# Seven half-size block products in place of eight in two feed-forward layers

## The chip, the cores and the metric

The kernel runs as one program on one core of one Trainium2 chip. The core has a matrix engine (TensorE; PE in the rows, PEld where it loads weights), a vector engine (DVE), a scalar engine (ACT), a general engine (POOL) and a queue engine (SP) that issues most of the transfers from device memory. Each engine works through its own instructions in their order and waits for the others by semaphores. Matmul results land in PSUM, which has eight banks of 128 x 512 fp32; everything else the engines touch lies in SBUF. The metric is the device time of one execution in microseconds (us).

## The reference: what is computed

Three transformer blocks run one after the other on 512 tokens of width 1024, in fp32. Each ends in a feed-forward layer of inner width 2816. The change touches that of block 2 (its second one) and that of block 3:

```python
def swiglu(h, w1, w2):                       # block 2
    g, u = jnp.split(h @ w1, 2, axis=-1)
    return (jax.nn.silu(g) * u) @ w2

def swiglu_3(u, w_gate, w_up, w_down):       # block 3
    return (jax.nn.silu(u @ w_gate) * (u @ w_up)) @ w_down

s = s + 0.5 * gate * swiglu(modulate(rmsnorm(s, nw), shift, scale), w1, w2)     # block 2
h = h + swiglu_3(rmsnorm_3(h, ffn_norm_g[l]), w_gate[l], w_up[l], w_down[l])    # block 3
```

## The kernel before

Activations lie with the channel on the 128 partitions and the 512 tokens along the row: a width of 1024 is eight tiles of 128 x 512. Every fp32 operand of a product is split in two: `hi`, the value cast to the matmul type fp32r (ACT), and `lo`, what the cast left (DVE, `lo = x - hi`). One product is then three matmuls (`mm3`, L280 to L282): hi by hi, hi by lo, lo by hi.

The up and gate projections go by pairs: `ffn` takes one tile of 128 gate channels and one of 128 up channels at a time, 22 pairs, in two parts of 11. For a pair, `wpair` (through `wload`, L260 to L265) brings 1 MB of weights as the tile `raw` (two buffers), and splits it into two chunks `wh`/`wl` of 128 x 1024 (three buffers each, `HL`). `gemm8` then makes each of the two 128 x 512 outputs from 8 x 3 matmuls of 512 columns in one PSUM bank. In block 2 ACT applies silu to the gate (L950), DVE multiplies by the up half (L951), and the result is split into the pair `g` (L318, L319). In block 3 (`kind` 3) both outputs are first multiplied by `A3`, the norm's factor per token (L954, L955). After 11 pairs the down projection runs: eight outputs of 11 x 3 matmuls of 512 columns, with weights through `wst`; then the other 11 pairs and the down projection again.

The activations `h` are eight hi/lo pairs of 128 x 512. In block 2 `modulated` makes them after the norm's statistics: a multiplication on DVE (L505), the cast with a shift on ACT (L508), the rest on DVE (L509), tile after tile. In block 3 `scaled` (L1557, L1558) makes them as the residual tiles of the projection before come out, since A3 is applied later.

A scheduler places the instructions of all engines by priority and dependence before the program runs; their order within an engine is then fixed. Tiles with few buffers decide how far one pair can run ahead of another.

## Time and profile before

| | us |
|---|---|
| median of 3 runs | 3245.63 (3242.1 to 3245.69) |
| the profiled execution | 3247.38 |
| its span, first to last instruction | 3245.4 |
| up and gate loads of block 2's layer, first to last issue | 2130.1 to 2436.5 |
| up and gate loads of block 3's layer, first to last issue | 2812.6 to 3130.7 |

In the rows, an instruction stands with its engine, the line of the kernel that issued it, its operation, and `out<-in` by the program's tile names (mm and x are PSUM banks, h the activations, wh and wl the weights' halves, raw the weights as loaded, tmp and ny scratch). Columns of a matmul are the second number of its shape. A busy PE is not a measure of its speed, because recorded matmuls overlap: what one costs is the distance between two starts.

### The profile page before, as it was taken

Reading aid. Unit: us, or ns where it says so; the run is one execution under the profiler, and the core shown is the slowest. Engines: PE = TensorE matmul, PEld = TensorE weight load, DVE = VectorE, ACT = ScalarE, POOL = GpSimd, SP = SyncE. Lnnn points to the kernel's source line nnn. Section 1 sums busy time; section 2 is a strip of 40 time slices with the busy share of each in tenths; the row PEclk is TensorE's granted clock in tenths of the full one; section 3 lists DMA queues with packets and bytes.
Section 4 is the critical chain, followed back from the end, with each engine's and each line's share of the span. In section 5 each row is a group of like instructions: output and inputs, shape, how many; then the busy total and the mean of one; then the engine's idle time right before and its main releaser. Section 6 shows DMA issues by size and latency. Waiting matters only on the chain.

```text
span 3245.4 us, 40565 instructions
## 1 busy us (share of the span) xinstructions
PE 3168.7 (98%) x15785; PEld 2608.5 (80%) x15785; DVE 2152.6 (66%) x3835; ACT 1202.7 (37%) x1891; POOL 46.7 (1%) x127
## 2 busy tenths in 40 slices
PE   8999999998999999999999999899999999999998
PEld 4888888888888889888888787678888877888886
DVE  6999697769775668765638766763334798454343
ACT  3343333435443335422225433532223327432222
POOL 0000000001000000000000000000000001100000
PEclk9999999999999999999999999999999999999999
DMA  6434433353635335554524211022222220022322
GB/s 241 153 122 132 135 129 99 110 183 124 204 132 160 109 114 175 167 173 146 184 88 162 78 65 53 16 89 90 94 99 85 92 69 27 27 91 84 105 84 79
DMA packets 117296, 370.37 MB, mean 114 GB/s; under 512 B 11120, under 2 KB 13680, under 8 KB 114672
## 3 DMA queue, kind: packets, MB, share of 16 engines
q1 hardware_dynamic: 108576, 356.21, 32.9%
q10 hardware_dynamic: 8528, 11.57, 1.1%
q8 instruction: 124, 2.03, 0.3%
q14 instruction: 68, 0.56, 0.1%
HBM read 365.64 MB, written 2.10 MB: 113 GB/s over the span
## 4 chain that ended last, share of the span: by engine, by line
PE 88%; DVE 6%; ACT 2%; DMA 2%; issue 1%; ACTq 0%; POOL 0%; DVEq 0%; POOLq 0%
PE mm L280 25%; PE mm L282 25%; PE mm L281 25%; DVE wl L265 2%; PE x L852 1%; PE mm L1634 1%; PE mm L825 1%; PE mm L824 1%; PE mm L826 1%; PE x L1286 1%; PE x L427 1%; PE x L1608 1%; PE mm L365 1%; PE x L435 1%; ACT wh L264 1%
## 5 line engine op out<-in xcount | busy, mean ns | idle before, releaser
L264 ACT CAST wh<-raw 128x1024 fp32r<-128x1024 f32 (+2 forms) x583 | 567.7, 975 | 1485.0 <-PE mm L281 1066.1
L280 PE MATMUL mm<-h,wh 128*128 128x512 f32 (+1 forms) x2488 | 976.7, 393 | 8.1 <-ACT hv L1249 2.1
L282 PE MATMUL mm<-h,wl 128*128 128x512 f32 (+1 forms) x2488 | 971.0, 390 | 1.8 <-DVE wl L265 1.8
L281 PE MATMUL mm<-h,wh 128*128 128x512 f32 (+1 forms) x2488 | 966.5, 389 | 1.1 <-DVE h L502 1.1
L265 DVE TENSOR_TENSOR wl<-raw,wh 128x1024 fp32r<-128x1024 f32 (+2 forms) x583 | 657.7, 1129 | 368.7 <-ACT wh L264 362.1
L280 PEld LDWEIGHTS mm<-h,wh 128*128 128x128 f32 x2488 | 469.5, 189 | 107.7 <-ACT hv L1249 2.6
L282 PEld LDWEIGHTS mm<-h,wl 128*128 128x128 f32 x2488 | 468.5, 188 | 106.8 <-DVE wl L265 3.1
L281 PEld LDWEIGHTS mm<-h,wh 128*128 128x128 f32 x2488 | 468.7, 188 | 102.0 <-DVE h L502 1.6
L282 PE MATMUL mm<-g,wl 128*128 128x512 f32 (+1 forms) x880 | 328.9, 374 | 2.3 <-DVE wl L265 2.2
L280 PE MATMUL mm<-g,wh 128*128 128x512 f32 (+1 forms) x880 | 329.1, 374 | 0.2 <-ACT wh L264 0.2
L281 PE MATMUL mm<-g,wh 128*128 128x512 f32 (+1 forms) x880 | 328.3, 373 | 0.0
L342 DVE SCALAR_TENSOR_TENSOR acc<-graw,cs,acc 128x512 f32<-128x512 f32 x252 | 186.2, 747 | 105.7 <-DMA graw<-w_mod 91.3
L282 PEld LDWEIGHTS mm<-g,wl 128*128 128x128 f32 x880 | 165.7, 188 | 35.6 <-DVE wl L265 3.3
L280 PEld LDWEIGHTS mm<-g,wh 128*128 128x128 f32 x880 | 165.7, 188 | 32.4 <-ACT wh L264 0.4
L281 PEld LDWEIGHTS mm<-g,wh 128*128 128x128 f32 x880 | 165.8, 188 | 32.0
L874 DVE SCALAR_TENSOR_TENSOR ca<-ap,pv,ca 128x512 f32<-128x512 f32 x232 | 173.2, 747 | 6.1 <-ACT ca L866 3.7
L280 PE MATMUL mm<-hc,wh 128*128 128x256 f32 x440 | 125.3, 285 | 4.5 <-DVE tmp L951 4.5
L281 PE MATMUL mm<-hc,wh 128*128 128x256 f32 x440 | 125.5, 285 | 0.0
L282 PE MATMUL mm<-hc,wl 128*128 128x256 f32 x440 | 125.1, 284 | 0.0
L951 DVE TENSOR_TENSOR tmp<-tmp,mm 128x512 f32<-128x512 f32 (+1 forms) x66 | 39.1, 596 | 99.8 <-PE mm L282 99.1
L280 PEld LDWEIGHTS mm<-hc,wh 128*128 128x128 f32 x440 | 84.0, 191 | 4.8 <-DVE tmp L951 4.7
L318 ACT CAST g<-tmp 128x512 fp32r<-128x512 f32 (+1 forms) x110 | 63.3, 577 | 63.5 <-DVE tmp L951 30.5
(596 smaller groups left out, 3941.8 us busy)
## 6 DMA issues: line engine op xcount, KB each, us to landing
graw<-w_mod SPq DMA_DIRECT2D x192, 256.0 KB, 3.1
raw<-f1u SPq DMA_DIRECT2D x44, 1024.0 KB, 5.0
raw<-w1s SPq DMA_DIRECT2D x32, 1024.0 KB, 5.0
raw<-f1d SPq DMA_DIRECT2D x32, 704.0 KB, 4.2
raw<-wup SPq DMA_DIRECT2D x22, 1024.0 KB, 5.0
raw<-f2u SPq DMA_DIRECT2D x22, 1024.0 KB, 4.9
raw<-f3u SPq DMA_DIRECT2D x22, 1024.0 KB, 4.9
raw<-w2s SPq DMA_DIRECT2D x17, 1024.0 KB, 4.9
```

What stands on the lines that cost most here:

```text
L264: nc.scalar.copy(hi[:, :cn], raw[:, c0:c0 + cn])
L265: nc.vector.tensor_sub(lo[:, :cn], raw[:, c0:c0 + cn], hi[:, :cn].bitcast(F32))
L280: mm(ps, hi, xh, start=first, stop=False)
L281: mm(ps, hi, xl, start=False, stop=False)
L282: mm(ps, lo, xh, start=False, stop=last)
L318: s.nc.scalar.copy(hi, src)
L342: nc.vector.scalar_tensor_tensor(accs[i], src, vec[:, k:k + 1], accs[i], op0=ALU.mult, op1=ALU.add)
L365: nc.tensor.matmul(ps, vec[:, k:k + 1], raw[:, q * 512:(q + 1) * 512], start=k == 0, stop=k == KD - 1)
L427: nc.tensor.matmul(ps[:, j * P:(j + 1) * P], col[:, j:j + 1].to_broadcast([P, P]), s.ident, start=True, stop=True)
L435: nc.tensor.transpose(ps[:, j * P:(j + 1) * P], x[:, j * P:(j + 1) * P], s.ident)
L874: nc.vector.scalar_tensor_tensor(ca, ap[:, i:i + T], s.v("conv_w", 8 * i + j), ca, op0=ALU.mult, op1=ALU.add)
L951: nc.vector.tensor_mul(sg, sg, pb)
```

## The change

The 2 x 2 block form of the product is used: the weights of a pair are four blocks (gate tile and up tile, each by the lower and upper half of the 1024 input channels), the activations four (lower and upper half of the channels, first and second 256 tokens). Strassen's scheme in Winograd's form gets the four output blocks from seven block products instead of eight, with sums of blocks before and after.

- `seven_in` makes seven sets of activations for each of four channel-tile pairs (b11, b21, t1, t2, m3, t4, m22; 128 x 256, hi and lo): four POOL subtractions of 256 columns, casts on ACT, remainders on DVE. It takes the place of `modulated` in block 2 and of `scaled` in block 3.
- `seven_weights` makes four sums s1 to s4 of the weight blocks by four POOL additions of 128 x 512 a pair, into `ws` (s2, s3) and `wt` (s1, s4), which have one buffer each, and splits seven blocks of 512 columns in four chunks: [a1 a2], [s2 s3], [b2 s1], [s4]. The three `wh` and three `wl` buffers stay.
- `seven` makes the seven products, each of 4 x 3 matmuls of 256 columns, and combines them on DVE (L1045 to L1052 of the new code) with one copy on ACT (`p1`, L1044).
- In block 3 the up half is multiplied by A3 on POOL (L944), the gate half on DVE (L943).

```diff
--- before.py
+++ after.py
@@ -937,6 +937,15 @@
         for i in range(NH):
             s.bg(bg(i))
             j = part * NH + i
+            if isinstance(h[0], dict):
+                sg, bt = s.seven(s.lp, w1, 2 * j, h)
+                if kind == 3:
+                    nc.vector.tensor_mul(sg, sg, s.A3)
+                    nc.gpsimd.tensor_mul(bt, bt, s.A3)
+                nc.scalar.activation(sg, sg, AF.Silu)
+                nc.vector.tensor_mul(sg, sg, bt)
+                g.append(s.split(sg, pool, "g", 2 * NH + 2, n))
+                continue
             w = s.wpair(w1, 2 * j)
             pa, pb = s.gemm8(w[0], h, n), s.gemm8(w[1], h, n)
             if kind == 1:
@@ -962,6 +971,86 @@
             for hi, lo, k, c in s.wst(w2, m, part * NH, NH):
                 s.mm3(ps, hi[:, c:c + P], lo[:, c:c + P], g[k][0], g[k][1], k == 0, k == NH - 1)
             out(m, ps)
+
+
+    HB = T // 2
+
+    def seven_in(s, pool, tp, y0, y1):
+
+        nc, g, H = s.nc, s.nc.gpsimd, s.HB
+        a, b = slice(0, H), slice(H, T)
+        (bh, bl), (th, tl) = s.hpair(), s.hpair()
+        mh, ml = (pool.tile([P, 3, H], F32R, tag="hs", name=s.nm("hs"), bufs=8) for _ in range(2))
+        t = tp.tile([P, 4, H], F32, tag="tt", name=s.nm("tt"), bufs=2)
+        nc.scalar.copy(bh[:, a], y0[:, a])
+        nc.vector.tensor_sub(bl[:, a], y0[:, a], bh[:, a].bitcast(F32))
+        g.tensor_sub(t[:, 1, :], y0[:, b], y0[:, a])
+        g.tensor_sub(t[:, 0, :], y1[:, b], t[:, 1, :])
+        g.tensor_sub(t[:, 2, :], y0[:, b], y1[:, b])
+        g.tensor_sub(t[:, 3, :], y1[:, a], t[:, 0, :])
+        t01, t23 = (t[:, i:i + 2, :].rearrange("p a f -> p (a f)") for i in (0, 2))
+        nc.scalar.copy(th, t01)
+        nc.vector.tensor_sub(tl, t01, th.bitcast(F32))
+        nc.scalar.copy(bh[:, b], y1[:, a])
+        nc.vector.tensor_sub(bl[:, b], y1[:, a], bh[:, b].bitcast(F32))
+        m01h, m01l = (m[:, 0:2, :].rearrange("p a f -> p (a f)") for m in (mh, ml))
+        nc.scalar.copy(m01h, t23)
+        nc.vector.tensor_sub(m01l, t23, m01h.bitcast(F32))
+        nc.scalar.activation(mh[:, 2, :], y1[:, b], AF.Copy, scale=-1.0)
+        nc.vector.scalar_tensor_tensor(ml[:, 2, :], y1[:, b], -1.0, mh[:, 2, :].bitcast(F32), op0=ALU.mult, op1=ALU.subtract)
+        return {"b11": (bh[:, a], bl[:, a]), "b21": (bh[:, b], bl[:, b]), "t2": (th[:, a], tl[:, a]), "t1": (th[:, b], tl[:, b]),
+                "m3": (mh[:, 0, :], ml[:, 0, :]), "t4": (mh[:, 1, :], ml[:, 1, :]), "m22": (mh[:, 2, :], ml[:, 2, :])}
+
+    def seven_weights(s, pool, name, mt):
+
+        nc, g = s.nc, s.nc.gpsimd
+        raw = s.wp.tile([P, 2048], F32, tag="raw", name=s.nm("raw"), bufs=2)
+        nc.sync.dma_start(raw.rearrange("p (m f) -> p m f", m=2), s.a[name][mt:mt + 2].rearrange("m p f -> p m f"))
+        a1, a2, b1, b2 = (raw[:, 512 * i:512 * i + 512] for i in range(4))
+        ws = pool.tile([P, 1024], F32, tag="ws", name=s.nm("ws"), bufs=1)
+        wt = pool.tile([P, 1024], F32, tag="wt", name=s.nm("wt"), bufs=1)
+        s2, s3, s1, s4 = ws[:, 0:512], ws[:, 512:1024], wt[:, 0:512], wt[:, 512:1024]
+        g.tensor_add(s1, b1, b2)
+        g.tensor_add(s2, a1, s1)
+        g.tensor_add(s3, a1, b1)
+        g.tensor_add(s4, a2, s2)
+        out = []
+        for parts in ([raw[:, 0:1024]], [ws], [b2, s1], [s4]):
+            hi = s.wp.tile([P, 1024], F32R, tag="wh", name=s.nm("wh"), bufs=HL)
+            lo = s.wp.tile([P, 1024], F32R, tag="wl", name=s.nm("wl"), bufs=HL)
+            c = 0
+            for src in parts:
+                n = src.shape[1]
+                nc.scalar.copy(hi[:, c:c + n], src)
+                nc.vector.tensor_sub(lo[:, c:c + n], src, hi[:, c:c + n].bitcast(F32))
+                c += n
+            out += [(hi, lo, o) for o in range(0, c, 512)]
+        return out
+
+    def seven(s, pool, name, mt, hs):
+
+        nc, V, H = s.nc, s.nc.vector, s.HB
+        a1, a2, s2, s3, b2, s1, s4 = s.seven_weights(pool, name, mt)
+        def prod(ps, w, mv):
+            hi, lo, o = w
+            for k in range(4):
+                c = o + k * P
+                s.mm3(ps, hi[:, c:c + P], lo[:, c:c + P], *hs[k][mv], k == 0, k == 3)
+            return ps
+        p1 = pool.tile([P, H], F32, tag="p1", name=s.nm("p1"), bufs=2)
+        at = s.tmp()
+        bt = pool.tile([P, T], F32, tag="bt", name=s.nm("bt"), bufs=2)
+        u, v = at[:, H:], bt[:, H:]
+        nc.scalar.copy(p1, prod(s.psm((P, H)), a1, "b11"))
+        V.tensor_sub(u, p1, prod(s.psx((P, H)), s2, "t2"))
+        V.tensor_add(at[:, 0:H], p1, prod(s.psm((P, H)), a2, "b21"))
+        V.tensor_sub(v, prod(s.psx((P, H)), s3, "m3"), u)
+        V.tensor_add(bt[:, 0:H], v, prod(s.psm((P, H)), b2, "t4"))
+        q = prod(s.psx((P, H)), s1, "t1")
+        V.tensor_add(v, v, q)
+        V.tensor_sub(u, u, q)
+        V.tensor_sub(u, u, prod(s.psm((P, H)), s4, "m22"))
+        return at, bt
 
     def dwconv3(s, pool, ps, j, n):
         nc = s.nc
@@ -1524,7 +1613,6 @@
         nc, tc = s.nc, s.tc
         A, _ = s.stats(acc["sq"], None, EPS2)
         sc = s.scw("scl3", s.v("n3w", 0, 8), s.modL[:, 56:64])
-        h = s.modulated(x, A, None, sc, s.modL[:, 48:56])
         hg = s.half_gate("hgl3", s.modL[:, 64:72])
         w = s.ct([P, 8], "w3")
         nc.vector.tensor_mul(w, s.v("fn2", 0, 8), s.v("an3", 0, 8))
@@ -1535,8 +1623,20 @@
             s.accum_w(acc, k, x[k], s.v("fn2", k))
             s.u.append(s.scaled(x[k], w[:, k:k + 1], NM))
         with tc.tile_pool(name="f3", bufs=1, reuse_waits="tile") as pool:
+            h = []
+            with tc.tile_pool(name="f3i", bufs=1, reuse_waits="tile") as tp:
+                for k in range(4):
+                    y = []
+                    for i in (k, k + 4):
+                        y.append(tp.tile([P, T], F32, tag="yy", name=s.nm("yy"), bufs=4))
+                        nc.vector.scalar_tensor_tensor(y[-1], x[i], sc[:, i:i + 1], A, op0=ALU.mult, op1=ALU.mult)
+                        nc.scalar.activation(y[-1], y[-1], AF.Identity, scale=1.0, bias=s.modL[:, 48 + i:49 + i])
+                    h.append(s.seven_in(pool, tp, *y))
+            s.lpc = tc.tile_pool(name="f3s", bufs=1, reuse_waits="tile")
+            s.lp = s.lpc.__enter__()
             s.ffn(pool, h, T, "f2u", "f2d", 2, s.part(x, hg), 0)
             s.ffn(pool, h, T, "f2u", "f2d", 2, out, 1)
+            s.lpc.__exit__(None, None, None)
         return x, acc
 
     def accum_w(s, acc, k, x, w):
@@ -1649,17 +1749,27 @@
             s.mixer3(pool, x, acc)
             acc = {}
             s.proj2("wo3", 1, s.o[4:8], s.part(x, 1.0, acc))
-        h = [s.scaled(x[k], s.v("ffn3", k)) for k in range(KD)]
         with tc.tile_pool(name="f4", bufs=1, reuse_waits="tile") as pool:
+            h = []
+            with tc.tile_pool(name="f4i", bufs=1, reuse_waits="tile") as tp:
+                for k in range(4):
+                    y = []
+                    for i in (k, k + 4):
+                        y.append(tp.tile([P, T], F32, tag="yy", name=s.nm("yy"), bufs=4))
+                        nc.scalar.activation(y[-1], x[i], AF.Copy, scale=s.v("ffn3", i))
+                    h.append(s.seven_in(pool, tp, *y))
             A, _ = s.stats(acc["sq"], None, EPS2)
             s.A3 = pool.tile([P, T], F32, tag="A3", name="A3")
             nc.scalar.copy(s.A3, A)
+            s.lpc = tc.tile_pool(name="f4s", bufs=1, reuse_waits="tile")
+            s.lp = s.lpc.__enter__()
             acc = {}
             def fin(k, ps):
                 s.resid(x[k], ps, 1.0, acc, k)
                 nc.scalar.activation(x[k], x[k], AF.Copy, scale=s.v("fn3", k))
             s.ffn(pool, h, T, "f3u", "f3d", 3, s.part(x, 1.0), 0)
             s.ffn(pool, h, T, "f3u", "f3d", 3, fin, 1)
+            s.lpc.__exit__(None, None, None)
         A, _ = s.stats(acc["sq"], None, EPS2)
         for k in range(KD):
             nc.vector.tensor_mul(x[k], x[k], A)
```

On DVE a pair of block 2 before is four rows. They stand here from the sixth pair on, with what surrounds them; wl is the remainder of a weight chunk, tmp the gated product, g its remainder:

```order
L319 TENSOR_TENSOR g_18167<-tmp_18163,g_18166 128x512
L265 TENSOR_TENSOR wl_18244<-raw_18237,wh_18243 128x1024
L951 TENSOR_TENSOR tmp_18230<-tmp_18230,mm_18205 128x512
L265 TENSOR_TENSOR wl_18307<-raw_18304,wh_18306 128x1024
L319 TENSOR_TENSOR g_18234<-tmp_18230,g_18233 128x512
L265 TENSOR_TENSOR wl_18311<-raw_18304,wh_18310 128x1024
L951 TENSOR_TENSOR tmp_18297<-tmp_18297,mm_18272 128x512
```

The same place now: the combination of one pair (tmp and bt are its two outputs, p its copied first product) lies between the remainders of the next pair's weights:

```order
L1046 TENSOR_TENSOR tmp_18666<-p_3383_18665,mm_18696 128x256
L1025 TENSOR_TENSOR wl_18662<-wt_18642,wh_18661 128x512
L1047 TENSOR_TENSOR bt_18667<-x_18710,tmp_18666 128x256
L1025 TENSOR_TENSOR wl_18782<-raw_18773,wh_18781 128x1024
L1048 TENSOR_TENSOR bt_18667<-bt_18667,mm_18724 128x256
L1050 TENSOR_TENSOR bt_18667<-bt_18667,x_18738 128x256
L1051 TENSOR_TENSOR tmp_18666<-tmp_18666,x_18738 128x256
L1025 TENSOR_TENSOR wl_18786<-ws_18775,wh_18785 128x1024
L1052 TENSOR_TENSOR tmp_18666<-tmp_18666,mm_18753 128x256
L1025 TENSOR_TENSOR wl_18790<-raw_18773,wh_18789 128x512
L1025 TENSOR_TENSOR wl_18790<-wt_18776,wh_18789 128x512
L946 TENSOR_TENSOR tmp_18666<-tmp_18666,bt_18667 128x512
```

In place of two weight remainders of 1024 columns stand two of 1024 and three of 512, and seven subtractions and additions of 256 columns that read PSUM (mm, x); L1045 and the remainder of the pair before's g (L319) stand just ahead of these rows.

POOL has no instruction in the up and gate stages before; its last rows ahead of block 3's attention are fills:

```order
L1385 MEMSET mqz_17060 64x512
L1385 MEMSET mqz_17174 64x512
L1385 MEMSET mqz_17317 64x512
L1385 MEMSET mqz_17460 64x512
L1680 MEMSET cm 128x400
```

Now it makes the sums of each pair. In block 3 the rows of two pairs read (bt is the up half of the pair before):

```order
L944 TENSOR_TENSOR bt_26275<-bt_26275,A_25290 128x512
L1015 TENSOR_TENSOR ws_26521<-raw_26519 128x512
L1013 TENSOR_TENSOR wt_26522<-raw_26519 128x512
L1014 TENSOR_TENSOR ws_26521<-raw_26519,wt_26522 128x512
L1016 TENSOR_TENSOR wt_26522<-raw_26519,ws_26521 128x512
L944 TENSOR_TENSOR bt_26411<-bt_26411,A_25290 128x512
L1015 TENSOR_TENSOR ws_26657<-raw_26655 128x512
L1013 TENSOR_TENSOR wt_26658<-raw_26655 128x512
L1014 TENSOR_TENSOR ws_26657<-raw_26655,wt_26658 128x512
L1016 TENSOR_TENSOR wt_26658<-raw_26655,ws_26657 128x512
```

The first sum of a pair waits for the remainders that read `ws` or `wt` of the pair before, and the sums follow one another by a semaphore. The A3 multiplication of one pair stands behind the sums of the next.

## Rows read from the trace of the kernel before

**Rows 1.** The page: busy time of each engine, its share, instructions

```profile
PE 3168.7 (98%) x15785; PEld 2608.5 (80%) x15785; DVE 2152.6 (66%) x3835; ACT 1202.7 (37%) x1891; POOL 46.7 (1%) x127
```

**Rows 2.** Chain that ended last, shares of the span

```profile
PE 88%; DVE 6%; ACT 2%; DMA 2%; issue 1%; ACTq 0%; POOL 0%; DVEq 0%; POOLq 0%
```

**Rows 3.** Timeline of PE (start, length), block 2's up and gate stage

```profile
2180.19 0.39 PE L282 MATMUL mm<-h,wl 128*128 128x512 f32 x1
...
2189.87 0.39 PE L282 MATMUL mm<-h,wl 128*128 128x512 f32 x1
```

**Rows 4.** Timeline of PE, a stage with 256 columns

```profile
832.49 0.28 PE L282 MATMUL mm<-hc,wl 128*128 128x256 f32 x1
...
837.89 0.28 PE L280 MATMUL mm<-g,wh 128*128 128x256 f32 x1
```

**Rows 5.** Timeline of DVE, one pair of block 2's stage

```profile
2190.37 0.69 DVE L951 TENSOR_TENSOR tmp<-tmp,mm 128x512 f32<-128x512 f32 x1 [3.46 <-PE mm L282]
2191.20 1.23 DVE L265 TENSOR_TENSOR wl<-raw,wh 128x1024 fp32r<-128x1024 f32 x1
2192.34 0.68 DVE L319 TENSOR_TENSOR g<-tmp,g 128x512 fp32r<-128x512 f32 x1
...
2201.41 0.69 DVE L951 TENSOR_TENSOR tmp<-tmp,mm 128x512 f32<-128x512 f32 x1 [3.46 <-PE mm L282]
```

**Rows 6.** Groups by form: busy, mean ns of one

```profile
L951 DVE TENSOR_TENSOR tmp<-tmp,mm 128x256 f32<-128x256 f32 x22 | 9.0, 415 | 1.5 <-PE mm L282 1.5
...
L264 ACT CAST wh<-raw 128x1024 fp32r<-128x1024 f32 x422 | 442.3, 1049 | 1096.2 <-PE mm L281 749.0 <-issue 246.8 <-PE mm L826 41.9
...
L318 ACT CAST g<-tmp 128x512 fp32r<-128x512 f32 x88 | 54.6, 621 | 61.3 <-DVE tmp L951 28.4 <-DVE tmp L957 18.3 <-DVE tmp L947 13.7
```

**Rows 7.** Timeline of DVE, instructions that follow without a wait

```profile
2860.94 0.68 DVE L989 SCALAR_TENSOR_TENSOR xr<-mm,xr 128x512 f32<-128x512 f32 x1
2861.54 0.74 DVE L1558 SCALAR_TENSOR_TENSOR h<-xr,pv,h 128x512 fp32r<-128x512 f32 x1
2862.20 1.21 DVE L265 TENSOR_TENSOR wl<-raw,wh 128x1024 fp32r<-128x1024 f32 x1
2863.33 0.68 DVE L483 TENSOR_TENSOR asq<-asq,tmp 128x512 f32<-128x512 f32 x1
```

**Rows 8.** Timeline of DVE beside a POOL addition

```profile
718.35 0.75 DVE L705 SCALAR_TENSOR_TENSOR gx<-xr,pv,gx 128x512 f32<-128x512 f32 x1
719.02 1.79 DVE L705 SCALAR_TENSOR_TENSOR ggx<-xr,lnc,ggx 128x512 f32<-128x512 f32 x1
```

**Rows 9.** Timeline of POOL, the same stretch

```profile
718.46 1.79 POOL L703 TENSOR_TENSOR sm<-sm,xr 128x512 f32<-128x512 f32 x1 [4.70 <-DVE xr L630]
```

**Rows 10.** Line L705, its middle instruction: ns min/median/max

```profile
L705 DVE SCALAR_TENSOR_TENSOR ggx<-xr,lnc,ggx x7: 1761/1789/1799, 719.0 to 755.9; 128x512 f32<-128x512 f32 x7
```

**Rows 11.** Timeline of DVE, start of block 2's stage

```profile
2164.10 2.06 DVE L505 SCALAR_TENSOR_TENSOR ny<-xr,scl,x 128x512 f32<-128x512 f32 x3 [2.17 <-PE x L427]
```

**Rows 12.** Timeline of DVE, first pair of block 3's stage

```profile
2873.50 0.69 DVE L955 TENSOR_TENSOR tmp<-mm,A 128x512 f32<-128x512 f32 x1 [3.30 <-PE mm L282]
```

**Rows 13.** Stretches: us, PE, PEld, DVE, ACT, POOL busy, PEclk, DMA share, GB/s

```profile
2156.00:2158.00 2.00, 0.00 (x0) 0.00 (x0) 1.91 (x3) 1.08 (x2) 0.00 (x0) 1.00 0.25 100
...
2160.00:2162.00 2.00, 0.02 (x1) 0.02 (x1) 1.62 (x10) 0.00 (x0) 0.00 (x0) 0.57 0.00 0
...
2640.00:2700.00 60.00, 55.73 (x241) 41.39 (x240) 58.20 (x153) 21.63 (x38) 3.45 (x9) 1.00 0.23 75
```

**Rows 14.** Timeline of PE at the low clock

```profile
2167.10 0.63 PE L281 MATMUL mm<-h,wh 128*128 128x512 f32 x1
2167.53 0.63 PE L282 MATMUL mm<-h,wl 128*128 128x512 f32 x1
```

**Rows 15.** Issues: KB each, us to landing

```profile
raw<-f2u SPq DMA_DIRECT2D x22, 1024.0 KB, 4.9
```

## The prediction

> **What bounds the kernel now.** I read the busy times first. PE is busy 98% of the span, DVE 66%, ACT 37%, POOL 1% [rows 1]; the chain that ended last runs through PE for 88% [rows 2]. So time is won on PE alone, and as long as the others keep up. Then the starts on PE. In the stage that the change touches, 42 matmuls of 512 columns lie between the two rows, 9.68 us: 0.2305 each [rows 3]. With 256 columns, 46 steps take 5.40 us: 0.1174 each [rows 4]. Half the columns cost 51%, so smaller blocks lose almost nothing on PE. Last the other engines in one pair: L951 starts every 11.04 us after waiting 3.46 us for PE [rows 5], and 48 x 0.2305 = 11.06. PE sets the pace of a pair, and DVE and POOL are mostly idle beside it.
>
> **PE's part.** A pair goes from 48 matmuls of 512 columns to 7 x 12 = 84 of 256: 84 x 0.1174 = 9.86 us. That is 1.20 us less a pair, 53 us over 44 pairs, if PE still sets the pace. The down projections do not change. A product takes 12 x 0.1174 = 1.41 us.
>
> **What DVE and POOL get.** Recorded lengths overlap the next start, so I take starts: a DVE instruction of 512 columns takes 0.60, the three-operand form 0.66, one of 1024 columns 1.13 [rows 7]. One of 256 that reads PSUM is recorded as 0.415 [rows 6], so about 0.34 with the same 0.08 off. Before, a pair has two of 1024 and two of 512, 3.5 us. Now it has two of 1024, five of 512 and seven of 256: 2.26 + 3.00 + 2.38 = 7.6 us, in block 3 one more of 512, 8.2. Against 9.86 this alone would fit. ACT: two casts at 1.05, five instructions of 512 at about 0.62, one copy of 256: 5.6 us [rows 6], which fits too. The loads are the same 22 of 1 MB, landing in 4.9 us [rows 15] in two buffers that come free half a pair ahead; they cost nothing.
>
> POOL is the open price. The trace has one such case: an addition of 128 x 512 lasts 1.79 us there [rows 9]. Beside it stand two DVE instructions with two SBUF operands: the first, 0.75, had begun just before; the second lasts 1.79 instead of 0.75 [rows 8], the same seven times out of seven, 1761 to 1799 ns [rows 10]. The two engines shut each other out: POOL waits until 719.10, when the first ends, runs until 720.25, and the second DVE instruction stands still for 1.04. So the addition alone costs 1.04 to 1.15 us by this reading, and 1.80 if POOL did not wait itself. I take 1.10, where both lengths fit, and keep 1.04 and 1.80 as ends. POOL then has 4.4 us a pair, in block 3 5.5, in which no DVE instruction with two SBUF operands runs. Those are 5.3 us a pair (5.9 in block 3). Together 9.7 and 11.4: block 3's pairs cannot go faster than before by this alone.
>
> The Trainium skill (SBUF — State Buffer, section "SBUF: two separate sides") says that the port shared by the two engines is held for a whole instruction, and that against a POOL instruction reading SBUF a DVE one needs it only with two SBUF inputs. By that rule the seven combinations that read PSUM would run beside POOL and the sum stays as below; no run here shows it, and the opposite is priced as the second rival.
>
> **The loop.** One buffer each for ws and wt and the fixed order tie the pairs in a ring. I follow it in block 2 from the end of the remainder of s4 of one pair, with 0.05 between engines. POOL makes s1 of the next pair until 1.2. The remainder of [a1 a2] has waited and now holds the port until 2.3; then s2 until 3.4. ACT casts [s2 s3] until 4.5, and its remainder (1.22) ends at 5.8, s4 running beside the cast. Only now can PE make that pair's second product. L1052 ends at 6.1; POOL meanwhile took the port for the pair after's s3 until 7.0. The remainders of b2 and s1 and the product with silu (L946) end at 8.9, the cast of g at 9.55, its remainder at 10.2, L1046 at 10.5, the remainder of s4 at 11.2. That is longer than PE's 9.86, so PE waits about 1.3 us a pair and a pair takes 11.2 instead of 11.04. Block 3 has two more steps in the ring: the A3 multiplication on DVE (0.6) and on POOL (1.1), both on two SBUF operands: 12.9.
>
> 20 of each block's 22 pairs follow another one (10 in each part): block 2 20 x 0.16 = +3, block 3 20 x 1.86 = +37. The second parts begin with weights prepared during the down projection: 2 x -1.2 = -2.
>
> **The starts.** Block 2's tiles of h start at 2164.10 [rows 11] and feed PE one by one; its first pair ends at 2190.37 - 11.04 = 2179.3 [rows 5]. Now every product needs all four tile pairs. DVE has 8 x 0.66 + 8 x 0.60 + 8 x 0.34 + 4 x 0.40 = 14.4 us; POOL has 16 subtractions of 256 columns, at half of 1.10 8.8 us, against 9.1 of DVE on the same port: between 14.4 and 23.2. With two to four buffers the tile pairs wait for each other, so 20. Behind it come three sums (3.3), cast and remainder (2.3), and the five products not made meanwhile (7.0): the pair ends near 2196.7, 17 us later. In block 3 the last residual tile ends at 2861.6 [rows 7] and the first pair's second output is read at 2873.50 [rows 12]. Now about 7 us of DVE and 4.4 of POOL still stand behind that tile, say 10, then again 5.6 and 7.0: 2884.2, 11 us later. Bounds for both: +14 to +45.
>
> **Sum.** +3 + 37 - 2 + 17 + 11 = +66 us on the profiled execution's 3247.4: 3313.5. The median of the runs shown is 1.8 below that execution, so 3312 for a median.
>
> **Rivals.**
> - PE sets the pace and the change is faster. It holds if POOL and DVE do not shut each other out, or POOL adds faster than here. The ring without that is 1.2 + 1.1 + 1.1 + 1.3 + 0.3 + 1.2 + 0.7 + 0.7 + 0.6 + 0.3 + 0.7 = 9.2, under PE's 9.86; it decides from there. Then -53 + 18 for the starts: about 3211. For it: DVE's 7.6 us fits. Against it: [rows 8 to 10], seven times alike. 0.12.
> - DVE's PSUM instructions are shut out too, or POOL is slower than 1.10. The combinations then wait for s2 and s4 (+1.0) and L1052 for s3 (+0.2): rings of 12.4 and 14.1, 20 x 1.36 + 20 x 3.06 - 2 + 33 = +119: 3365. With 1.80 for an addition the rings are 13.3 and 15.7 and the starts 45: +45 + 93 - 2 + 45 = +181, 3427. Nothing in the trace speaks against the first. 0.20.
> - The ring hides better than I walk it, and only the port's own sum and PE hold: 9.9 and 11.4 a pair, 20 x -1.14 + 20 x 0.36 - 2 + 22 = +4: 3250. 0.14.
> - PE's pauses bring its clock down to 1.2 GHz. PE made nothing from 2156 to 2158 and little up to 2162; there the granted clock is 1.00 first and then 0.57, on its way from 2.4 to 1.2 GHz [rows 13], and behind it matmuls of 512 columns stand 0.43 apart [rows 14], so some 0.215 for 256: 84 x 0.215 = 18.1, +7.0 x 44 = +308, 3554. Against it: a stretch with PE busy 55.7 of 60 us keeps 1.00 [rows 13], and the ring leaves pauses of 1.3 us. 0.03.
>
> That the change does not do what it says is no rival: the order shows the 84 matmuls and the sums in place.
>
> **How the numbers follow.** My case has 0.51, with a range of its own of 3285 to 3345 (starts +14 to +45, rings 0.3 shorter or 0.4 longer). The wide range reaches down to 3250 and up to the second rival's first time and some way on, 3395; it leaves out the fast rival and the upper ends. A measurement of this kernel can tell about 0.2%, 6.5 us, from no change. Faster by more: 0.12 and a fifth of the third rival, 0.15. Within: a third of that rival, 0.05. Slower: the rest, 0.80.
>
> **What would show it.** In the changed profile: matmuls of 256 columns 0.117 apart within a product; the remainder of [s2 s3] as PE's releaser once a pair, with pauses of 1 to 1.5 us in block 2 and near 3 in block 3; POOL additions of 1.1 to 2.2 us, and DVE remainders stretched by about 1 us beside them; L1052 starting every 11.2 and 12.9 us. DVE and POOL busy with PE never waiting for them, and 9.9 between two pairs, would prove me wrong.

## The result and the profile after

The changed kernel takes 3330.68 us (median of 4 runs, 3327.26 to 3332.61) against 3245.05 us for the kernel before on the same chip: a ratio of 1.0265, 95% interval 1.0247 to 1.0282. It is slower by 85.6 us, where 66 had been forecast. The profiled execution has a span of 3330.4 us against 3245.4.

The busy times and the shares of the chain that ended last, from the page of the kernel after; they answer to [rows 1, 2]:

```profile
PE 3163.1 (95%) x17369; PEld 2670.3 (80%) x17369; DVE 2446.4 (73%) x4277; ACT 1303.6 (39%) x2107; POOL 390.6 (12%) x357
...
PE 73%; DVE 13%; POOL 4%; ACT 4%; issue 4%; DMA 2%; ACTq 0%; DVEq 0%; POOLq 0%
```

PE has lost 15 points of the chain, and DVE, POOL, ACT and "issue" (time in which an engine waits for nothing that the profile shows) stand in it instead. Where in the program, a table tells. Its borders are the first DVE instruction of block 2's last feed-forward layer, the first and last remainder of a tile of g (L319) of each part, and the last remainder of a tile of h (L319) in block 3's mixer. For example, block 2's start in the kernel after is 2204.20 - 2164.02 = 40.2. The first border lies between 2155.6 (e10) and 2168.9 (e1) in the profiles shown here, so the stages of two profiles are compared and not their spans.

| us | start of block 2 | 1st part | between | 2nd part | down, then mixer of block 3 | start of block 3 | 1st part | between | 2nd part | end | sum |
|---|---|---|---|---|---|---|---|---|---|---|---|
| before | 18.8 | 108.3 | 73.4 | 110.0 | 363.5 | 38.0 | 110.8 | 72.5 | 110.8 | 75.3 | 1081.3 |
| after | 40.2 | 111.3 | 74.3 | 111.7 | 373.3 | 60.5 | 123.1 | 74.5 | 124.0 | 73.6 | 1166.4 |
| difference | 21.4 | 3.0 | 0.9 | 1.7 | 9.8 | 22.5 | 12.3 | 2.0 | 13.2 | -1.7 | 85.1 |

So 44 us go into the two starts, 30 into the pairs, and 10 into a stage in which not one line was changed.

**PE within the products.** Two rows of PE in the changed kernel, to be set against [rows 3, 4]: 70 matmuls lie from the first to the second, 8.22 us, so 0.1174 each, as forecast.

```profile
2967.91 0.28 PE L280 MATMUL x<-h,wh 128*128 128x256 f32 x1
...
2976.13 0.28 PE L281 MATMUL mm<-h,wh 128*128 128x256 f32 x1
```

**One pair of block 2.** Instructions of DVE, POOL and ACT, and one of PE, in order of time (start, duration, engine, line; in brackets the idle time before and its releaser); L1013 to L1016 are the sums s1, s2, s3 and s4, L1025 the remainders of the weights, L1052 is the last combination. The last two rows are L1052 in block 3:

```profile
2239.45 0.68 DVE L1025 TENSOR_TENSOR wl<-wt,wh 128x512 fp32r<-128x512 f32 x1
...
2240.22 1.29 POOL L1013 TENSOR_TENSOR wt<-raw 128x512 f32<-128x512 f32 x1 [4.15 <-DVE wl L1025]
2240.39 2.20 DVE L1025 TENSOR_TENSOR wl<-raw,wh 128x1024 fp32r<-128x1024 f32 x1
2241.58 2.16 POOL L1014 TENSOR_TENSOR ws<-raw,wt 128x512 f32<-128x512 f32 x1
2242.51 0.41 DVE L1048 TENSOR_TENSOR bt<-bt,mm 128x256 f32<-128x256 f32 x1
...
2243.78 1.05 ACT L1024 CAST wh<-ws 128x1024 fp32r<-128x1024 f32 x1 [3.77 <-POOL ws L1014]
2243.82 1.29 POOL L1016 TENSOR_TENSOR wt<-raw,ws 128x512 f32<-128x512 f32 x1
...
2244.85 1.34 DVE L1025 TENSOR_TENSOR wl<-ws,wh 128x1024 fp32r<-128x1024 f32 x1 [1.07 <-ACT wh L1024]
...
2246.12 0.41 DVE L1052 TENSOR_TENSOR tmp<-tmp,mm 128x256 f32<-128x256 f32 x1
2246.25 0.39 PE L282 MATMUL x<-h,wl 128*128 128x256 f32 x1 [0.87 <-DVE wl L1025]
2246.32 1.29 POOL L1015 TENSOR_TENSOR ws<-raw 128x512 f32<-128x512 f32 x1 [1.21 <-issue]
2246.45 1.72 DVE L1025 TENSOR_TENSOR wl<-raw,wh 128x512 fp32r<-128x512 f32 x1
...
2954.36 0.41 DVE L1052 TENSOR_TENSOR tmp<-tmp,mm 128x256 f32<-128x256 f32 x1
...
2967.56 0.41 DVE L1052 TENSOR_TENSOR tmp<-tmp,mm 128x256 f32<-128x256 f32 x1
```

Read it as the ring of the prediction. The remainder of s4 (2239.45) frees wt, POOL makes s1 (2240.22); the remainder of [a1 a2] gets the port behind it and lasts 2.20 where it lasts 1.22 alone; s2 in its turn lasts 2.16; the cast of [s2 s3] and its remainder follow, and L1052 closes the pair. But L1048, which reads PSUM, runs its usual 0.41 while s2 is still being made (2241.58 to 2243.74). It is no single case: all 44 of L1048 last 0.405 to 0.415, and 39 of them lie wholly inside the record of a POOL instruction. A POOL sum that does not have to wait for DVE lasts 1.29, not 1.10. PE waits for the remainder of [s2 s3] once a pair, 0.87 us here; all its pauses of more than 0.2 us come to 1.1 us a pair in block 2 and 2.0 in block 3, where 1 to 1.5 and near 3 had been forecast. DVE itself is idle for 1.5 us a pair. L1052 starts every 11.54 us in block 2, and in block 3 every 12.94 as a rule (13.20 in the rows shown); the last pair of each part, with no follower whose sums stand in its way, takes only 8.7 and 9.9.

**The stage that was not changed.** ACT's queue at the start of block 3's mixer: the load of the rope table and that of the meta tokens, and the first instruction that needs the latter. In the kernel before the two loads are issued at 2116.15 and 2119.43, during block 2's mixer:

```profile
2560.14 0.33 ACTq L1787 DMA_DIRECT2D tab<-rope  x1
...
2561.47 0.45 ACTq L1795 DMA_DIRECT2D xm<-metaT  x1
...
2568.27 0.31 ACT L1797 ACTIVATE sqm<-xm 128x128 f32<-128x128 f32 x1 [5.32 <-DMA xm<-metaT]
```

Busy time of the engines in a 4 us stretch there (PE, its weight loads, DVE, ACT, POOL, the granted clock, DMA share, GB/s):

```profile
2563.00:2567.00 4.00, 0.00 (x0) 0.00 (x0) 1.29 (x3) 0.00 (x0) 0.00 (x0) 0.50 0.92 319
```

PE makes nothing, the DMA engines are 92% busy, and PE's granted clock is at 0.50, 1.2 GHz, when work comes back.

**The starts.** Busy time in block 2's start, the same columns:

```profile
2160.00:2170.00 10.00, 4.03 (x12) 2.86 (x12) 6.67 (x18) 4.43 (x9) 3.51 (x5) 0.50 0.01 2
2170.00:2180.00 10.00, 5.29 (x14) 3.50 (x14) 10.00 (x16) 6.79 (x15) 6.36 (x8) 0.50 0.00 0
2180.00:2190.00 10.00, 2.75 (x7) 1.58 (x7) 5.85 (x9) 4.24 (x9) 8.95 (x8) 0.50 0.00 0
2190.00:2200.00 10.00, 10.00 (x68) 9.78 (x69) 8.70 (x11) 4.43 (x7) 6.58 (x5) 0.80 0.30 105
```

From 2170 to 2180 DVE is the one that is full, from 2180 to 2190 POOL; then the first pair's products run, part of the time at the low clock.

### The profile page after: what moved, and what is told of

Read it like the earlier page. It is cut to its first block, busy times and chain, and to the rows that moved or that the text cites. A ratio compares the mean times of both kernels' runs of the same rounds, so it can differ in the third digit from the quotient of the medians.

```text
span 3330.4 us, 44924 instructions
## 1 busy us (share of the span) xinstructions
PE 3163.1 (95%) x17369; PEld 2670.3 (80%) x17369; DVE 2446.4 (73%) x4277; ACT 1303.6 (39%) x2107; POOL 390.6 (12%) x357
## 4 chain that ended last, share of the span: by engine, by line
PE 73%; DVE 13%; POOL 4%; ACT 4%; issue 4%; DMA 2%; ACTq 0%; DVEq 0%; POOLq 0%
PE mm L280 19%; PE mm L282 19%; PE mm L281 19%; DVE wl L1025 3%; POOL ws L1014 2%; DVE wl L265 2%; POOL wt L1013 1%; ACT wh L1024 1%; PE x L852 1%; PE mm L1734 1%; PE mm L825 1%; PE mm L824 1%; PE mm L826 1%; PE x L427 1%; PE x L1375 1%
## 5 line engine op out<-in xcount | busy, mean ns | idle before, releaser
L264 ACT CAST wh<-raw 128x1024 fp32r<-128x1024 f32 (+2 forms) x495 | 475.1, 962 | 1170.4 <-PE mm L281 902.6
L280 PE MATMUL mm<-h,wh 128*128 128x512 f32 (+2 forms) x2136 | 803.4, 377 | 15.7 <-ACT h L985 6.7
L282 PE MATMUL mm<-h,wl 128*128 128x512 f32 (+2 forms) x2136 | 799.5, 374 | 10.7 <-DVE wl L1025 8.7
L281 PE MATMUL mm<-h,wh 128*128 128x512 f32 (+2 forms) x2136 | 797.2, 373 | 7.3 <-DVE h L986 4.3
L265 DVE TENSOR_TENSOR wl<-raw,wh 128x1024 fp32r<-128x1024 f32 (+2 forms) x495 | 553.3, 1119 | 279.7 <-ACT wh L264 276.2
L280 PEld LDWEIGHTS mm<-h,wh 128*128 128x128 f32 x2136 | 406.9, 191 | 88.3 <-ACT h L985 8.1
L282 PEld LDWEIGHTS mm<-h,wl 128*128 128x128 f32 x2136 | 406.5, 190 | 88.0 <-DVE wl L1025 11.6
L281 PEld LDWEIGHTS mm<-h,wh 128*128 128x128 f32 x2136 | 406.6, 190 | 82.4 <-DVE h L986 6.3
L1025 DVE TENSOR_TENSOR wl<-raw,wh 128x1024 fp32r<-128x1024 f32 x88 | 154.0, 1750 | 2.9 <-ACT wh L1024 2.5
L282 PE MATMUL x<-h,wl 128*128 128x256 f32 x352 | 104.8, 298 | 32.0 <-DVE wl L1025 31.7
L280 PE MATMUL mm<-hc,wh 128*128 128x256 f32 x440 | 125.2, 285 | 4.5 <-DVE tmp L960 4.5
L281 PE MATMUL mm<-hc,wh 128*128 128x256 f32 x440 | 125.2, 285 | 0.0
L280 PE MATMUL x<-h,wh 128*128 128x256 f32 x352 | 104.4, 297 | 21.3 <-ACT wh L1024 21.0
```

What stands on the lines that cost most here:

```text
L264: nc.scalar.copy(hi[:, :cn], raw[:, c0:c0 + cn])
L265: nc.vector.tensor_sub(lo[:, :cn], raw[:, c0:c0 + cn], hi[:, :cn].bitcast(F32))
L280: mm(ps, hi, xh, start=first, stop=False)
L281: mm(ps, hi, xl, start=False, stop=False)
L282: mm(ps, lo, xh, start=False, stop=last)
L1025: nc.vector.tensor_sub(lo[:, c:c + n], src, hi[:, c:c + n].bitcast(F32))
```

## The experiments

Each was timed beside the kernel before on the same chip; ratios are to the kernel before. Its stages, measured like the table above:

| us | start 2 | 1st | between | 2nd | mixer | start 3 | 1st | between | 2nd | end | sum |
|---|---|---|---|---|---|---|---|---|---|---|---|
| e1, no sums | 35.2 | 93.4 | 72.3 | 98.6 | 373.3 | 54.7 | 97.8 | 72.6 | 100.2 | 73.8 | 1072.1 |
| e2, two wt | 42.9 | 115.4 | 75.6 | 116.8 | 373.2 | 64.2 | 130.4 | 75.9 | 131.3 | 73.9 | 1199.6 |
| e3, sums on DVE | 38.2 | 101.2 | 72.8 | 101.6 | 371.5 | 58.1 | 117.1 | 71.7 | 114.6 | 72.6 | 1119.5 |
| e4, block 2 only | 40.3 | 111.4 | 74.3 | 111.7 | 373.6 | 38.5 | 111.3 | 72.5 | 111.3 | 75.7 | 1120.7 |
| e6, tables early | 40.2 | 111.3 | 74.3 | 111.6 | 368.2 | 59.3 | 122.8 | 74.5 | 125.2 | 73.9 | 1161.3 |
| e7, before + room | 18.7 | 108.3 | 73.3 | 110.0 | 372.2 | 37.0 | 110.8 | 72.5 | 110.8 | 75.7 | 1089.2 |
| e8, three sums on DVE | 39.7 | 98.6 | 72.6 | 98.3 | 368.0 | 58.6 | 110.2 | 73.1 | 111.5 | 74.0 | 1104.6 |
| e9, A3 too | 39.7 | 98.6 | 72.6 | 98.3 | 368.0 | 57.8 | 111.5 | 71.0 | 113.7 | 73.2 | 1104.5 |
| e10, subtractions on DVE | 39.5 | 111.4 | 74.3 | 111.6 | 371.9 | 58.2 | 124.1 | 74.8 | 123.9 | 73.7 | 1163.4 |
| e11, block 2, best form | 36.7 | 98.7 | 72.6 | 98.3 | 369.3 | 37.2 | 111.3 | 72.5 | 111.3 | 75.2 | 1083.1 |

### e1: the sums left out

```diff
-        ws = pool.tile([P, 1024], F32, tag="ws", name=s.nm("ws"), bufs=1)
-        wt = pool.tile([P, 1024], F32, tag="wt", name=s.nm("wt"), bufs=1)
-        s2, s3, s1, s4 = ws[:, 0:512], ws[:, 512:1024], wt[:, 0:512], wt[:, 512:1024]
-        g.tensor_add(s1, b1, b2)
-        g.tensor_add(s2, a1, s1)
-        g.tensor_add(s3, a1, b1)
-        g.tensor_add(s4, a2, s2)
+        ws, s1, s4 = raw[:, 1024:2048], b1, a1
```

> This kernel is the changed one without the four weight sums on POOL: raw weight blocks stand in their place, so its output is not the reference's; products, casts, remainders and combinations stay, and so does the A3 multiplication on POOL in block 3. Theory (a ring through POOL's sums, and POOL and DVE shutting each other out): block 2 goes from 11.54 to PE's 9.9 us a pair, block 3 from 12.94 to 9.9 to 10.5; about 18 and 16 pairs of each block run at the full period, so -29 and -44, and about -8 for the sums in the two starts: 3250 +-12 against the changed kernel's 3331. Rival (DVE's fixed order with its seven combinations and single buffers binds by itself): pairs stay above 11.2 and 12, the time above 3310.

Measured: 3234.24 us, ratio 0.997 (0.9961 to 0.998). The last combination starts every 9.92 us in block 2 and every 10.12 in block 3. Two stretches of 20 us, in block 2 and block 3 of this kernel:

```profile
2240.00:2260.00 20.00, 20.00 (x172) 20.00 (x171) 16.49 (x29) 10.79 (x16) 0.00 (x0) 1.00 0.32 106
2940.00:2960.00 20.00, 20.00 (x168) 19.65 (x167) 18.25 (x31) 10.57 (x16) 2.51 (x2) 1.00 0.29 104
```

PE is never idle and POOL's column is empty in block 2. So there the sums on POOL, with what waits for them, are the whole price of the pairs, and DVE's longer list is not; in block 3 0.2 us a pair are left. The time lies below the 3238 to 3262 expected: the four parts gained 80 us on the changed kernel and the starts 11, where 73 and 8 had been reckoned. Against the kernel before the parts gain 50 us; the starts, still 16 to 17 longer each, eat 33 of them and the stage of the tables 10.

### e2: two buffers for wt

```diff
-        wt = pool.tile([P, 1024], F32, tag="wt", name=s.nm("wt"), bufs=1)
+        wt = pool.tile([P, 1024], F32, tag="wt", name=s.nm("wt"), bufs=2)
```

> The changed kernel with two buffers for wt (s1 and s4) instead of one. Theory (it is the ring, not the sum of the work, that sets the period): s1 of the next pair no longer waits for the remainder of s4, and what is left is the port's sum, 5.3 + 4 x 1.29 = 10.5 us a pair in block 2 and 5.9 + 5 x 1.29 = 12.3 in block 3: 18 x -1.04 and 16 x -0.64, so -29: 3302. Rival (the two engines' sum on the port, stretched as it is, is already the whole period): 11.5 and 12.9 stay, 3331 +-5.

Measured: 3361.37 us, ratio 1.036 (1.0342 to 1.0377). Theory and rival were both wrong: it is 31 us slower than the changed kernel, and a pair takes 12.48 and 14.05. DVE and POOL in one pair of block 2 of this kernel:

```profile
2257.53 0.41 DVE L1052 TENSOR_TENSOR tmp<-tmp,mm 128x256 f32<-128x256 f32 x1
2257.86 1.74 DVE L1025 TENSOR_TENSOR wl<-raw,wh 128x512 fp32r<-128x512 f32 x1
2259.52 1.77 DVE L1025 TENSOR_TENSOR wl<-wt,wh 128x512 fp32r<-128x512 f32 x1
2261.22 1.78 DVE L946 TENSOR_TENSOR tmp<-tmp,bt 128x512 f32<-128x512 f32 x1
...
2265.56 2.20 DVE L1025 TENSOR_TENSOR wl<-raw,wh 128x1024 fp32r<-128x1024 f32 x1
```

```profile
2257.75 1.30 POOL L1014 TENSOR_TENSOR ws<-raw,wt 128x512 f32<-128x512 f32 x1 [3.54 <-DVE wl L1025]
2259.01 1.73 POOL L1015 TENSOR_TENSOR ws<-raw 128x512 f32<-128x512 f32 x1
2260.70 1.74 POOL L1016 TENSOR_TENSOR wt<-raw,ws 128x512 f32<-128x512 f32 x1
...
2265.39 1.30 POOL L1013 TENSOR_TENSOR wt<-raw 128x512 f32<-128x512 f32 x1 [2.94 <-DVE wl L1025]
```

With the ring broken, s2, s3 and s4 come in a row and meet three DVE instructions with two SBUF operands; each of these lasts 1.74 to 1.78 instead of 0.69. All four sums cost DVE about 1.05 each, and DVE is idle for 0.46 us of a pair only: 7.6 + 4 x 1.05 + 0.46 = 12.3 of the 12.48. In the changed kernel only two of the four do (the rows of 2.20 and 1.72); the other two fall where DVE reads PSUM or waits. So the theory is mended. In the changed kernel the ring binds, and DVE still waits for 1.5 us a pair; with the ring broken DVE's one queue binds, and the pair gets longer. In that queue a sum on POOL costs about 1 us when an instruction with two SBUF operands stands next to it, and nothing when none does. The ring gave the right length for this order, but it was also what kept the sums apart.

### e3: the sums on DVE

```diff
-                    nc.gpsimd.tensor_mul(bt, bt, s.A3)
+                    nc.vector.tensor_mul(bt, bt, s.A3)
...
-        g.tensor_add(s1, b1, b2)
...
-        g.tensor_add(s4, a2, s2)
+        nc.vector.tensor_add(s1, b1, b2)
...
+        nc.vector.tensor_add(s4, a2, s2)
```

> The changed kernel with the four sums and block 3's second A3 multiplication on DVE instead of POOL. Theory (mutual exclusion and POOL's 1.29 us a sum are the price): DVE has 7.6 + 4 x 0.60 = 10.0 us a pair in block 2 and 8.2 + 5 x 0.60 = 11.2 in block 3, nothing is shut out: pairs of 10.0 to 10.6 and 11.2 to 11.9, so -16 to -27 in each block and -4 in the starts: 3273 to 3295. Rival (DVE's own queue is what binds, and POOL's work mostly lies beside it): a pair gets up to 2.4 us longer, 3350 or more.

Measured: 3284.35 us, ratio 1.0127 (1.0112 to 1.0142), as the theory had it. Two instructions of DVE in this kernel, the first a sum:

```profile
2262.27 0.68 DVE L1015 TENSOR_TENSOR ws<-raw 128x512 f32<-128x512 f32 x1
2262.87 0.42 DVE L1047 TENSOR_TENSOR bt<-x,tmp 128x256 f32<-128x256 f32 x1
```

From start to start an addition costs DVE 0.60 of its own, against about 1.05 when POOL makes it beside one with two SBUF operands. Pairs settle at 10.5 in block 2 and 11.6 in block 3's second part, with DVE idle for 0.2 to 0.3 us of each. The first part of block 3 does something else: periods of 9.48 and 14.6 by turns. Windows of 2 us there:

```profile
2930.00:2932.00 2.00, 0.58 (x5) 0.38 (x4) 2.00 (x5) 0.47 (x1) 0.00 (x0) 1.00 0.00 0
2932.00:2934.00 2.00, 1.07 (x5) 0.86 (x6) 2.00 (x4) 2.00 (x4) 0.00 (x0) 0.82 0.00 0
2934.00:2936.00 2.00, 2.00 (x11) 2.00 (x11) 2.00 (x3) 0.75 (x2) 0.00 (x0) 0.50 0.04 8
2936.00:2938.00 2.00, 2.00 (x16) 2.00 (x16) 1.30 (x3) 0.37 (x1) 0.00 (x0) 0.83 0.14 12
```

PE was idle for 2.0 us (to 2932.6), made a few products, was idle for 0.3 more, and the granted clock went to 0.50, where 11 matmuls fall into the 2 us that have room for 17 at 0.1174.

### e6: the tables loaded early

```diff
+        s.tbc = tc.tile_pool(name="tb", bufs=1, side="right", reuse_waits="tile")
+        s.tb = s.tbc.__enter__()
+        s.tab = s.tb.tile([P, 4, TK], F32, tag="tab3", name="tab3")
+        nc.scalar.dma_start(s.tab, s.a["rope3"])
+        s.xm = s.tb.tile([P, KD, NM], F32, tag="xm", name="xm")
+        nc.scalar.dma_start(s.xm, s.a["metaT"].rearrange("k p t -> p k t"))
...
-                g.append(s.split(sg, pool, "g", 2 * NH + 2, n))
+                g.append(s.split(sg, pool, "g", 2 * NH, n))
```

The added lines stand at the beginning of block2_tail; the two loads in the mixer go. The last two lines take two buffers from g, so e6, and e8, e9 and e11 after it, differ from the changed kernel in that too.

> The changed kernel with the rope table and the meta tokens of block 3's mixer in a pool of their own on the other side of SBUF, loaded at the start of block 2's last feed-forward layer. Theory (in the changed kernel these two loads are issued only at 2560 because their SBUF room is taken by the larger layer pools, and PE, DVE and ACT wait for them): the 11.3 us that the changed kernel loses between 2535 and 2872 go away: 3320. Rival (that stretch is longer because PE's clock fell or DVE was behind, with the loads merely the last label): no gain, 3331 +-4.

Measured: 3323.79 us, ratio 1.0246 (1.0231 to 1.0261): 7 us faster than the changed kernel, less than the 11 expected. In the stage itself 373.3 goes to 368.2, so 5.1 of the 9.8 are gone. PE no longer waits for a load there, but still for DVE, twice in a row:

```profile
2573.30 1.16 PE L427 MATMUL x<-ident,r 128*128 128x128 f32 x8 [2.94 <-DVE r L1826]
...
2576.84 0.79 PE L280 MATMUL mm<-h,wh 128*128 128x512 f32 x1 [2.38 <-DVE ckv L1835]
```

```profile
2575.00:2582.00 7.00, 5.16 (x12) 4.09 (x13) 6.76 (x20) 0.93 (x3) 0.52 (x1) 0.53 0.00 0
```

In the kernel before only the second of these pauses is there, 1.27 us long, and the granted clock stays at 1.00 around it. So the 4.7 us that are left go with these pauses, about 4 us longer together, and with the 7 us at 0.50 behind them; why DVE comes late there is not shown.

### e7: the kernel before with room taken

```diff
+            s.room = pool.tile([P, 9216], F32, tag="room", name="room")
...
+            if k == KD - 1:
+                nc.gpsimd.tensor_copy(s.room[:, 0:T], x[k])
```

> The kernel before with one thing added: an unused tile of 36 kB a partition that holds SBUF room during block 2's last feed-forward layer (one small copy on POOL at its end touches it). Theory (room alone delays the rope table and the meta tokens): the loads are issued some 440 us later, at the start of block 3's mixer, and the time rises by 7 to 12: 3252 to 3257. Rival (it was not the loads): 3245 +-3.

Measured: 3253.39 us, ratio 1.003 (1.0019 to 1.0041). The kernel before, with nothing but an idle tile, loses 9.7 us, of which 8.7 in the very stage. ACT's queue in it:

```profile
2533.29 0.65 ACTq L1688 DMA_DIRECT2D xm<-metaT  x1
2537.47 0.31 ACT L1690 ACTIVATE sqm<-xm 128x128 f32<-128x128 f32 x1 [4.52 <-DMA xm<-metaT]
```

The load has moved from 2119 to 2533 and ACT waits for it. So room taken in SBUF is enough to move these loads and to cost most of the 9.8 us, without any arithmetic.

### e4: block 2 alone

The hunk on block 3 is taken back:

```diff
+        h = [s.scaled(x[k], s.v("ffn3", k)) for k in range(KD)]
         with tc.tile_pool(name="f4", bufs=1, reuse_waits="tile") as pool:
-            h = []
-            with tc.tile_pool(name="f4i", bufs=1, reuse_waits="tile") as tp:
...
```

> The change in block 2 alone; block 3 as before. Theory (the traces' differences stage by stage): block 2 +25.5, and +11.3 at the start of block 3's mixer because block 2's larger pools push the two loads behind it; block 3's own +48 go away: 3245 + 37 = 3282. Rival (the late loads come from block 3's pools or from the change as a whole): 3245 + 25.5 = 3271.

Measured: 3282.86 us, ratio 1.0119 (1.0106 to 1.0133). Block 2's pools alone push the tables back (373.6), and block 3 costs the remaining 48 us. The costs add up stage by stage.

### e8 and e9: s4 alone on POOL

```diff
-        g.tensor_add(s1, b1, b2)
-        g.tensor_add(s2, a1, s1)
-        g.tensor_add(s3, a1, b1)
+        nc.vector.tensor_add(s1, b1, b2)
+        nc.vector.tensor_add(s2, a1, s1)
+        nc.vector.tensor_add(s3, a1, b1)
```

Both have the tables as in e6; e9 has the A3 multiplication on DVE as in e3 besides.

> The changed kernel with the early tables of e6 and with s1, s2 and s3 on DVE; only s4, and block 3's second A3 multiplication, stay on POOL. After e2 the theory is: what a sum on POOL costs depends on what DVE has in its queue just then; beside instructions with two SBUF operands each costs DVE about 1.05 us, beside the combinations that read PSUM nothing. s4 starts when s2 is done, and three combinations (1.0 us) stand next on DVE: nearly free. DVE has 7.6 + 3 x 0.60 = 9.4 in block 2, 10.0 in block 3: pairs of 9.9 to 10.1 and 10.1 to 11.1, which is -30 and -30 to -49, tables -7, starts -8: 3237 to 3256. Rival (each POOL sum costs DVE its whole length wherever it falls, as in e2): 10.45 and 12.1 a pair, 3283.

> As e8, with block 3's second A3 multiplication on DVE too. Theory: it lies between two-operand instructions, so on POOL it costs 1.05 and on DVE 0.60: DVE 10.6 a pair in block 3, pairs of 10.7 to 11.0, 3240 to 3258; if e8's pair in block 3 is at 10.2 or less, e8 is the faster of the two by about 10. Rival (as for e8): 11.6 in block 3, about 3272.

Measured: e8 3270.98 us, ratio 1.0082 (1.0069 to 1.0094); e9 3269.58 us, 1.0075 (1.0063 to 1.0088). Both lie above the 3237 to 3258 that the theory gave, and e8 below its rival's 3283. In block 2 the mended theory holds: pairs of 10.03 and 9.91, PE never idle. POOL's s4 and the DVE instructions beside it there, in e8:

```profile
2248.91 1.30 POOL L1016 TENSOR_TENSOR wt<-raw,ws 128x512 f32<-128x512 f32 x1 [8.74 <-DVE ws L1014]
```

```profile
2249.03 0.42 DVE L1051 TENSOR_TENSOR tmp<-tmp,x 128x256 f32<-128x256 f32 x1
2249.77 0.42 DVE L1052 TENSOR_TENSOR tmp<-tmp,mm 128x256 f32<-128x256 f32 x1 [0.32 <-PE mm L282]
2250.11 1.22 DVE L1025 TENSOR_TENSOR wl<-ws,wh 128x1024 fp32r<-128x1024 f32 x1
```

The whole sum lies beside combinations that read PSUM, and no DVE instruction is stretched. In block 3 it was too hopeful: the pairs average 11.2 in e8, with a granted clock of 1.00, and 11.2 and 11.3 in e9. DVE's order is another there; s4 meets s3 on DVE (1.40 instead of 0.68 at 3132.37) and, in e8, the multiplication a remainder (1.96 instead of 1.22 at 3134.03). In e9 the multiplication by A3 costs DVE its own 0.60 and s4 goes on colliding. Both ways DVE is busy for 98 to 99% of the time, and the two kernels come out alike. That e8 would be the faster by 10 us had been expected only for pairs of 10.2 or less.

### e10 and e11: the starts, and the best form

```diff
-        g.tensor_sub(t[:, 1, :], y0[:, b], y0[:, a])
-        g.tensor_sub(t[:, 0, :], y1[:, b], t[:, 1, :])
-        g.tensor_sub(t[:, 2, :], y0[:, b], y1[:, b])
-        g.tensor_sub(t[:, 3, :], y1[:, a], t[:, 0, :])
+        nc.vector.tensor_sub(t[:, 1, :], y0[:, b], y0[:, a])
+        nc.vector.tensor_sub(t[:, 0, :], y1[:, b], t[:, 1, :])
+        nc.vector.tensor_sub(t[:, 2, :], y0[:, b], y1[:, b])
+        nc.vector.tensor_sub(t[:, 3, :], y1[:, a], t[:, 0, :])
```

e11 has this edit together with those of e8, and block 3 as before, as in e4.

> The changed kernel with the sixteen subtractions of 256 columns at each block's start (from y0 and y1) on DVE instead of POOL. Theory (mutual exclusion in the starts too): in block 2 DVE is occupied from 2164.0 to 2186.4, 22.4 us, of which 14.4 are its own and the rest stretches and waits for POOL; with 16 x 0.34 of its own in their place 19.8: 2.6 earlier in each start, 3326 (+-3). Rival (POOL's subtractions lie beside DVE for the most part): DVE gets 5.4 us more a start, of which 2 to 5 show: 3335 to 3341.

> The change in block 2 alone, with three of the four sums and the sixteen subtractions on DVE and the tables early: what the runs so far give as the best form. Theory: against the kernel before, block 2's two parts -21.3 (as in e8), its start +21.4 - 2.6, the mixer of block 3 +4.8 (what e6 left): 3246, no difference that can be measured. Rival (it beats the kernel before): only if the start costs under 13: below 3237.

Measured: e10 3325.08 us, ratio 1.0254 (1.024 to 1.0268); the time is the one expected, but by its stages it is only 3.0 us faster than the changed kernel, not 5 (0.7 in block 2's start, 2.3 in block 3's). DVE's 22.5 us for the tiles of h became 20.9 (19.8 reckoned), and the sums still stand on POOL behind them. e11 3248.21 us, ratio 1.0013 (1.0005 to 1.0022): the best form that the runs point to is level with the kernel before, and does not beat it. Only e1, which leaves out the sums and so does not compute the reference, is faster than the kernel before.

## Why the prediction was right, and where its sizes were off

**PE's part** held: 0.1174 a matmul in the changed kernel, and 9.92 a pair where nothing else stood in the way (e1).

**POOL and DVE shutting each other out** held, and so did its limit: L1048 read PSUM for 0.41 us in the middle of s2. The first form of the second rival falls by that row and the 43 like it. The Trainium skill (SBUF — State Buffer, section "SBUF: two separate sides") says that DVE takes the pair of ports it shares with POOL in a 2-port mode or, against a POOL instruction that reads SBUF, with two SBUF inputs. The trace agrees: L1048 has one SBUF input and keeps its 0.41. The size was off. From [rows 7 to 10] I took 1.10 for an addition; that is about the stretch of the DVE instruction (2.20 - 1.22 = 0.98, 1.72 - 0.68 = 1.04, in e2 up to 1.09). POOL's own length is 1.29, and it is this that stands in the ring, twice: 2 x 0.19 = +0.4, about the step from 11.2 to 11.54. Of the rival's other form, a slower POOL, a little came: 1.29, not its 1.80.

**The loop** gave 11.2 and 12.9; measured are 11.54 and 12.94, and the steps of the walk are the rows above. Two things failed in it. The count: the last pair of a part takes 8.7 and 9.9, so block 3 loses 25.5 (I had +37 and -1); in block 2 the longer ring outweighs the short last pairs, 4.7 (+3 and -1). And the reading: I took the single buffer for the cause that sets the price. It does set the order and the wait here, but e2 takes it away and the kernel gets slower, because the sums then collide with more of DVE's instructions. The cost that stays sits in DVE's queue.

**The starts** were sized at 17 and 11 and are 21.4 and 22.5. In block 2 the tiles of h were ready at 2186.5 against 2184 in the sum, the sums behind them lasted 1.71 twice beside DVE's remainders, and the five products took 9.0 us (2191.3 to 2200.3) instead of 7.0, with a granted clock of 0.50 before 2190 and 0.80 on average after. In block 3 the tiles took 11.3 us behind the last residual (10 reckoned), and the products 11.3 instead of 7.0, since POOL's work stretches the remainders between them (2.34 and 2.20 for 1024 columns). The sum had two terms at nothing there: the last residual itself comes 2.8 us later in the stage, and the way from L1052 to the first remainder of g takes 5.4 instead of the 2.5 from L955.

**"The loads ... cost nothing"** was the step that failed altogether. It looked at the weight loads and left out that larger pools take the room that loads of a later stage had used: 9.8 us, a tenth of the result. An idle tile alone costs 8.7 in that stage (e7), and loading the tables early brings back 5.1 (e6).

In sum 21.4 + 22.5 + 4.7 + 25.5 + 9.8 + 0.9 + 2.0 - 1.7 = 85.1, against 66 forecast: the pairs were reckoned 8 too dear, the starts 16 too cheap, the tables not at all. The way and the mechanism of the pairs were foreseen; that the total comes within 20 us is partly luck, since these errors offset one another.

**The rivals.** PE does not set the pace in the changed kernel. It does without the sums (e1) and, in block 2, with three of them on DVE (e8, e11). Even e1 takes 3234 and not 3211, since the starts cost 33 us together there, not 18, and the tables 10. The ring that hides better is excluded by the 11.54. The low clock through all pairs did not come. The granted clock is 1.00 in the rings of block 2. In block 3, where PE's pauses last 0.6 to 0.9 us, it falls to 0.50 four times, for 3 to 4 us each (near 2955, 3020, 3166 and 3218), for example:

```profile
3020.00:3023.00 3.00, 3.00 (x16) 3.00 (x15) 3.00 (x3) 0.20 (x1) 2.22 (x2) 0.50 0.26 33
```

PE has time to spare there: of the four pairs in which it falls, that of 2955 takes 13.20 us and the others keep their 12.93 to 12.95.

## What to carry to other kernels

An operation moved to POOL is not free because POOL is idle: look at what stands in DVE's queue at that moment, and give POOL only work that falls beside DVE instructions reading PSUM; for the others DVE's own 0.60 is cheaper here than the 1.05 it loses. An algorithm with fewer multiplications has to earn back its prologue first: here at most 1.1 us a pair (11.04 to 9.92) on 44 pairs against 22 us a block before the first tile of g. And when a pool grows, look through the later stages for loads that had been issued in its room.
